# A recurrence kernel: its first slots in another order, and one turn of carries behind the log of a denominator

## The chip, the cores and the metric

The kernel runs on one core of a Trainium2 chip. The metric is the device time of one execution in microseconds; of the kernel before, four runs have a median of 294.04 us (293.59 to 295.41). The profile shows one execution, which took 294.22 us; the instructions in it span 292.5 us.

## The reference

The inputs are `k` and `v`, both [16, 2048, 256] in float32, and two vectors `w` and `u` of length 256. For each of 16 batches and 256 channels a sum with decay runs over 2048 steps, kept in a form that cannot overflow:

```python
for t in range(seq_len):
    kk, vv = k[b, t, :], v[b, t, :]
    ww = u + kk
    qq = np.maximum(pp, ww)
    e1, e2 = np.exp(pp - qq), np.exp(ww - qq)
    output[b, t, :] = (e1 * aa + e2 * vv) / (e1 * bb + e2 + 1e-08)
    ww = pp - w + kk
    qq = np.maximum(ww, kk)
    e1, e2 = np.exp(ww - qq), np.exp(kk - qq)
    aa, bb, pp = e1 * aa + e2 * vv, e1 * bb + e2, qq
```

(Two statements are put on one line here in places.) Without the scaling by `pp`, `aa` is a decayed sum of exp(k)*v, `bb` the same sum of exp(k), and an output is a quotient of the two with the present step weighted by exp(u).

## The kernel before

**Tiling.** Time is cut into a head of 32 steps and 16 chunks of 126 (two halves of 63). A chunk lies on 126 partitions, one step on each, and is done in four pieces of four batches. The head is done in two pieces, `n` = 2 and 3, in which three groups of batches are stacked on 96 partitions. In all there are 66 pieces, numbered `n`: 0 and 1 are half of chunk 0, 2 and 3 the head, 4 and 5 the rest of chunk 0, 6 to 9 chunk 1, and so on.

**What is done with a piece.** `load` (L111) brings k through SP or POOL's queue and `load_v` (L136) brings v through POOL's, converted to bf16. `round_k` (L309, VectorE) copies k into a tile[...]. `logs` (L318, TensorE) multiplies it by two "step matrices" (NLE and NLZ, for the head NLEh and NLZh), which gives all exponents of the piece, X. `exps` (L339, ScalarE) takes their exponentials, `times_v` (L350, VectorE) multiplies them by v into the other half of the same tile, `ez`. `sums` (L375, TensorE) adds the piece to the totals of its chunk. Some slots later `den` (L549, TensorE) forms the denominators by triangular matrices (Lh and Lf) and identities (Id, It), `log_den` and `invert` (L561, L568, ScalarE) turn them into reciprocals, `num` and `mult` (L573, L585) form numerators and multiply, and `store` (L591, POOL's queue) writes.

**Carries.** When the totals of a chunk are complete, a chain of small operations, each put in a slot by the table PLANS (L625), turns the totals (`turn_sums`), takes logs, updates the state, and makes the carries into the chunk. `turn_carries` (L502) transposes them on TensorE into a PSUM bank of tag "den"; `inject` (L507) casts them to bf16 on VectorE (L509) and issues four DMAs of 8 KB on SP's queue (L513), which write them into rows 126 and 127 of the chunk's `ez` tiles; the first two go to the tile of the chunk's first two pieces. From piece 4 on `den` reads these rows. For chunk 1 the turn is in slot 12 at "p4" and the injection in slot 13 at "d0".

**Order.** Each engine works in the order in which instructions are written (K, L35, pins it). The main loop (L666) has a slot for each `n`: it starts the load of piece n+6 (`AHEAD`), takes the exponentials of n, rounds k of n+1, and later in the slot forms the logs of n+1, `times_v(n)` and `sums(n)`; small jobs run where `small_work(n, "d0")` and the like stand. `out_at` (L663) gives the slot in which a piece's denominators are formed: 6 slots later for the head, 10 for pieces 0 and 1, 9 for all others. So slots 8 to 11 serve pieces 2, 3, 0 and 1, slot 12 none, and slots 13, 14 and 15 pieces 4, 5 and 6. Until the end phase there is one PSUM buffer of tag "den"; `den`, `turn_sums` and `turn_carries` take it in turn. TensorE's `idle` matmuls on zeros fill gaps in the first nine slots. k and v each have six buffers, so that a load waits for the `round_k` or the `times_v` of the piece six before.

The constants of the head's step matrices and of the output matrices are built on VectorE in slots 0 to 2 (`matrices_for_head`, `matrices_for_outputs`, `matrices_for_outputs_of_head`, `more_matrices_for_outputs`).

Of the kernel before, what the change touches and what calls it, by code (L numbers as in the profile page):

```python
# [22 lines left out]
def kernel(  # L23
# [11 lines left out]
    def K(ins):  # L35

        block, e, new = nc.cur_bb.bb, ins.ins.engine, []
        for i in reversed(block.instructions):
            if i.engine == e:
                new.append(i)  # L40
                if i.name == pinned.get(e):
                    break
        for a, b in zip(new[1:], new):
            tc.add_manual_dep(b, a.name, mybir.DependencyInfo(
                mybir.DependencyClass.NoSync, mybir.DependencyReason.DATA), reason="order")
        pinned[e] = new[0].name
        return ins

    PE, DVE, SC, POOL, SP = nc.tensor, nc.vector, nc.scalar, nc.gpsimd, nc.sync
# [9 lines left out]
    NH = NG * GB  # L59
# [36 lines left out]
    def is_head(n):  # L96
        return pairs[n][0] < 0
# [5 lines left out]
    def tiles_of(n):  # L103
        return 1 if pairs[n] == (-1, 1) else 2
# [6 lines left out]
    def load(n):  # L111
        kr = kpool.tile([128, 4, Dm], F32, tag="kr", name="kr")
        vr = vpool.tile([128, 4, Dm], BF16, tag="vr", name="vr")
        kr_of[n], vr_of[n] = kr, vr
        c, p = pairs[n]
        if is_head(n):
            load_head(n, SP, kr, k)
        else:
            t0 = T0 + c * TC
            r = min(128, T - t0)  # L120
            K((SP if n < 2 else POOL).dma_start(  # L121
                out=kr[0:r, :, :], in_=k[4 * p:4 * p + 4, t0:t0 + r, :].rearrange("n t d -> t n d")))
            if n >= 2:
                load_v(n)

    def load_head(n, eng, t, x):
        p = pairs[n][1]
        for g in (0, 2, 1):
            b = 6 * g + 4 * p
            e = min(b + 2 * tiles_of(n), B)  # L130
            if b < e:
                K(eng.dma_start(out=t[g * GB:(g + 1) * GB, 0:e - b, :],
                                in_=x[b:e, 0:T0, :].rearrange("n t d -> t n d")))
# [39 lines left out]
    M1, I1, IO, IOh = [matrix(x, F32) for x in ("M1", "I1", "IO", "IOh")]  # L173
# [28 lines left out]
    NLE, NLZ, NLEh, NLZh = [matrix(x, F32R) for x in ("NLE", "NLZ", "NLEh", "NLZh")]  # L202

    def step_matrices(E, Z, rows, N, io):
        cw, cu = cc[:, rows:rows + 1], cc[:, rows + 1:rows + 2]
        K(DVE.scalar_tensor_tensor(E[:, 0:N], io[:, 0:N], cw, M1[:, 0:N], ALU.mult, ALU.add))
        K(DVE.scalar_tensor_tensor(Z[:, 0:N], I1[:, 0:N], cu, E[:, 0:N], ALU.add, ALU.add))
        K(DVE.tensor_scalar(E[:, 0:N], E[:, 0:N], cw, None, ALU.add))
# [51 lines left out]
    def matrices_for_sums():  # L260

        K(DVE.tensor_add(Ir[:, 0:16], I1[:, 0:16], I1[:, 32:48]))
        K(DVE.tensor_add(Ir[:, 16:32], I1[:, 64:80], I1[:, 96:112]))
        K(DVE.tensor_add(Ir[:, 32:48], I1[:, 16:32], I1[:, 48:64]))
        for t in (OHE, OHV):
            fill(t, 0.0)
            fill(t[0:HS, 8:9], 1.0)
            K(DVE.tensor_single_scalar(t[:, 16:17], cc[:, 4:5], 2.0, op=ALU.mult))
        K(DVE.tensor_copy(OHE[:, 24:33:8], cc[:, 2:4]))

    def matrices_for_head():
        step_matrices(NLEh, NLZh, 0, NH, IOh)
        for f in (NLEh, NLZh):
            head_blocks(f)
            fill(f[:, NH:128], 0.0)
        for g in range(NG):
            fill(NLEh[g * GB:(g + 1) * GB, NH + g:NH + g + 1], 0.5)
        K(DVE.tensor_single_scalar(NLEh[96:98, NH:NH + NG], cc[96:98, 0:1].broadcast_to([2, NG]),
                                   -0.5 * GB, op=ALU.mult))
# [29 lines left out]
    def round_k(n):  # L309
        r = NH if is_head(n) else TC  # L310
        i = 2 * tiles_of(n)
        if is_head(n):
            KM[n] = kmh.pop(0)
        else:
            KM[n] = kms[n % 2]
        K(DVE.tensor_copy(KM[n][0:r, 0:i, :], kr_of.pop(n)[0:r, 0:i, :]))  # L316

    def logs(n):  # L318
        kr = NH + 2 if is_head(n) else 128


        if n == HALVES:
            psx[0] = log_banks("psx")
        if n < HALVES:
            X = [psx[0].tile([128, 2, D], F32, tag=f"X{q}", name=f"X{q}") for q in range(2)]
        else:
            t = psx[0].tile([128, 2, 2, D], F32, tag="X", name="X")
            X = [t[:, 0], t[:, 1], t]
        km = KM.pop(n).rearrange("p (i n) d -> p i (n d)", i=2)
        for q, m in enumerate((NLEh, NLZh) if is_head(n) else (NLE, NLZ)):  # L330
            for i in range(tiles_of(n)):
                K(PE.matmul(X[q][:, i, :], m[0:kr, :], km[0:kr, i, :], start=True, stop=True))  # L332
        X_of[n] = X
# [16 lines left out]
    def times_v(n):  # L350
        ez = ez_of(n)
        i = tiles_of(n)
        r = NH if is_head(n) else TC
        vb = vr_of.pop(n)[:, 0:2 * i, :].rearrange("p (i n) d -> p i (n d)", n=2)
        K(DVE.tensor_mul(ez[0:r, 1:4:2], ez[0:r, 0:4:2],  # L355
                         vb[0:r].unsqueeze(1).broadcast_to([r, 2, i, D])))
# [261 lines left out]
    def at(slot, where, f, *args):  # L618
        later.setdefault((slot, where), []).append((f, args))

    def small_work(n, where):
        for f, args in later.pop((n, where), []):
            f(*args)
# [23 lines left out]
    for c in range(-1, NST):  # L647
        for slot, where, f, *args in PLANS["head" if c < 0 else "first" if c == 0 else
                                           "last" if c + 1 == NST else "steady"]:

            if f is copy_sums and 0 < c < NST - 1:
                where, args = "d1", (DVE,)
            at(last_of[c] + slot, where, f, c, *args)
    at(0, "d1", matrices_for_head)
    at(0, "d2", matrices_for_outputs)
    at(1, "d2", matrices_for_outputs_of_head)
    at(2, "d2", more_matrices_for_outputs)

    matrices_for_sums()
    round_k(0)  # L660
    logs(0)

    out_at = {n + (LAG - 3 if is_head(n) else LAG + 1 if n < 2 else LAG): n for n in range(NP)}  # L663
# [2 lines left out]
    for n in range(NP + LAG + 1):  # L666

        q, qi, qp = out_at.get(n), out_at.get(n - 1), out_at.get(n - 2)
        late = ([qp] if n == LATE else []) + [qi] if n >= LATE else []
        if n >= LATE:  # L670
            qp = None
        live, more, out_q, out_qi, out_qp = n < NP, n + 1 < NP, q is not None, qi is not None, qp is not None
        if n == NP:
            widen()
        if n + AHEAD < NP:
            load(n + AHEAD)
        small_work(n, "a3")
        if live:
            exps(n)
        small_work(n, "d0")  # L680
        if more:
            round_k(n + 1)
        small_work(n, "p0")
        if out_qp:
            num(qp, 0)
            if n > NP:
                num(qp, 1)
        small_work(n, "d1")
        small_work(n, "a0")
        small_work(n, "p1")  # L690
        if n == NP:
            num(qp, 1)
        if out_qi and qi < NP - 1:
            invert(qi)
        small_work(n, "a2")
        if out_q:
            if q not in DEN:
                den(q)
            if n == NP + 1:

                den(q + 1)
            if q < NP - 1:
                log_den(q)
            else:
                for i in range(2):
                    log_den(q, i, i + 1)
                    invert(q, i, i + 1)
        for x in late:
            num(x, 0)
            num(x, 1)  # L710
            mult(x, 0)
            mult(x, 1)
            store(x)
        if out_qp:
            mult(qp, 0)
        small_work(n, "d2")
        small_work(n, "d3")
        small_work(n, "a4")
        if more:
            logs(n + 1)  # L720
        if n < HALVES + 1:
            idle(psd if n < 5 else psn, 2)
        if live and out_qp:
            num(qp, 1)
        small_work(n, "p3")
        if live:
            times_v(n)
            sums(n)
        if n < HALVES + 1 and n != 4:
            idle(psd if n < 4 else psn, 2)  # L730
        small_work(n, "p2")
        small_work(n, "d4")
        if out_qp:
            mult(qp, 1)
            store(qp)
        small_work(n, "d5")
        small_work(n, "p4")
        small_work(n, "a1")
# [31 lines left out]
```

## Time and profile before

| | |
|---|---|
| median of four runs | 294.04 us (293.59 to 295.41) |
| profiled execution; span of its instructions | 294.22 us; 292.5 us |
| ScalarE (ACT) busy | 265.7 us, 91% of the span |
| VectorE (DVE) busy | 256.0 us, 88% |
| TensorE (PE) busy | 254.7 us, 87% |
| GpSimd (POOL) busy, most of it issuing DMAs | 161.4 us, 55% |
| HBM traffic | 68.12 MB read, 34.05 MB written |

In the profile, L12 is line 12 of the kernel; a group or a timeline row gives start and length in us, engine, line, operation, what it writes `<-` what it reads, the shape, how many (x), and in brackets how long the engine stood idle before it and who ended that. SPq and POOLq are the queues that issue DMAs. The landing of a DMA is the time of the last update of its semaphore. A table of windows gives the busy time of each engine in a stretch, with the number of instructions.

### The profile page before, as it was taken

The numbers are of one execution on the slowest core, as the hardware profiler recorded it, in microseconds if no ns is written. First come the engines' busy times: TensorE is split into PE (matmuls) and PEld (weight loads), VectorE is DVE, ScalarE is ACT, GpSimd is POOL, SyncE is SP. The second block draws the span as 40 slices with busy tenths as digits, with TensorE's granted clock in tenths as the row PEclk, the third lists the DMA queues.
The fourth block names the chain that finished last, engine by engine and source line by source line (L and its number), as shares of the span: only waits on it lengthen the run. The fifth ranks groups of instructions, "written<-read, shape, count | busy, mean of one in ns | idle before, by whom it ended". The sixth has DMA issues, their size and how long they took to land.

```text
span 292.5 us, 4134 instructions
## 1 busy us (share of the span) xinstructions
PE 254.7 (87%) x1210; PEld 118.9 (41%) x1210; DVE 256.0 (88%) x529; ACT 265.7 (91%) x298; POOL 161.4 (55%) x229
## 2 busy tenths in 40 slices
PE   7589988888989898989989899989899898988950
PEld 3235444443434443434444344444344444433420
DVE  5878899889999999999999999999999999978760
ACT  7569889799999999999999999999999999998970
POOL 8895447656555665555666555666465652212430
PEclk9999999999999999999999999999999999999995
DMA  5999999999999999999999999999999999445884
GB/s 180 228 265 298 308 306 274 223 331 326 319 322 329 338 327 333 318 335 344 341 324 327 334 337 339 336 323 332 336 318 335 324 296 284 148 148 185 280 251 148
DMA packets 58203, 85.95 MB, mean 294 GB/s; under 512 B 6746, under 2 KB 42066, under 8 KB 58180
## 3 DMA queue, kind: packets, MB, share of 16 engines
q0 software_dynamic: 52960, 83.04, 102.8%
q1 hardware_dynamic: 4922, 2.36, 3.2%
q10 hardware_dynamic: 298, 0.27, 0.3%
q8 instruction: 10, 0.16, 0.2%
q14 instruction: 13, 0.11, 0.1%
HBM read 68.12 MB, written 34.05 MB: 349 GB/s over the span
## 4 chain that ended last, share of the span: by engine, by line
DVE 39%; DMA 22%; PE 20%; issue 8%; ACT 8%; SPq 1%; DVEq 0%; ACTq 0%
DMA vr<-in_v_dram 17%; DVE ez L355 14%; DVE rd L589 10%; PE num L579 6%; DVE km L316 5%; PE X L332 4%; PE den L554 4%; ACT rd L566 3%; PE tot L386 3%; DMA ez<-row 2%; PE den L404 2%; DMA kr<-in_k_dram 2%; ACT ez L346 1%; DVE S L428 1%; ACT ez L348 1%
## 5 line engine op out<-in xcount | busy, mean ns | idle before, releaser
L348 ACT ACTIVATE ez<-X 128x2048 bf16<-128x2048 f32 x58 | 108.7, 1874 | 0.1
L143 POOL DMA_DIRECT2D vr<-in_v_dram x64 | 48.6, 759 | 80.3 <-DVE ez L355 42.2
L589 DVE TENSOR_TENSOR rd<-num,rd 128x512 f32<-128x512 f32 (+2 forms) x131 | 88.4, 682 | 4.4 <-ACT rd L571 3.6
L355 DVE TENSOR_TENSOR ez<-ez,vr 126x2048 bf16<-126x2048 bf16 (+1 forms) x66 | 79.7, 1207 | 2.1 <-ACT ez L346 2.1
L609 POOL DMA_DIRECT2D out_dram<-rd x63 | 55.0, 872 | 39.5 <-issue 10.6
L566 ACT ACTIVATE rd<-den 128x1024 f32<-128x1024 f32 (+3 forms) x67 | 66.9, 999 | 4.6 <-PE den L554 2.5
L571 ACT ACTIVATE rd<-rd 128x1024 f32<-128x1024 f32 (+3 forms) x67 | 69.3, 1035 | 0.3
L579 PE MATMUL num<-ez,LfN 128*128 128x512 bf16 (+1 forms) x128 | 49.2, 384 | 7.6 <-DVE rd L589 7.6
L332 PE MATMUL X<-km,NLE 128*128 128x512 f32 x128 | 50.3, 474 | 2.3 <-DVE km L316 1.9
L316 DVE CAST km<-kr 126x1024 fp32r<-126x1024 f32 x64 | 48.7, 761 | 2.2 <-DMA kr<-in_k_dram 2.2
L579 PE MATMUL num<-ez,IdN 126*128 126x512 bf16 (+1 forms) x131 | 49.8, 380 | 0.0
L121 POOL DMA_DIRECT2D kr<-in_k_dram x62 | 47.9, 773 | 1.4 <-DMA vr<-in_v_dram 0.5
L332 PE MATMUL X<-km,NLZ 128*128 128x512 f32 x128 | 40.4, 397 | 0.0
L554 PE MATMUL den<-ez,Id 126*128 126x512 bf16 (+1 forms) x131 | 39.1, 378 | 0.0
L554 PE MATMUL den<-ez,Lf 128*128 128x512 bf16 (+1 forms) x128 | 38.0, 378 | 0.6 <-DMA ez<-row 0.6
L386 PE MATMUL tot<-ez,OHV 126*32 126x512 bf16 x128 | 25.2, 384 | 6.4 <-DVE ez L355 6.3
L332 PEld LDWEIGHTS X<-km,NLE 128*128 128x128 f32 x128 | 23.0, 189 | 13.2 <-issue 1.4
L332 PEld LDWEIGHTS X<-km,NLZ 128*128 128x128 f32 x128 | 23.9, 188 | 6.1 <-ACT ez L346 0.6
L386 PE MATMUL tot<-ez,OHE 128*32 128x512 bf16 x128 | 25.2, 390 | 0.0
L579 PEld LDWEIGHTS <-LfN 128*128 128x128 bf16 (+1 forms) x128 | 12.3, 96 | 22.9 <-issue 20.5
L346 ACT ACTIVATE ez<-X 128x1024 bf16<-128x1024 f32 (+1 forms) x16 | 14.7, 971 | 6.8 <-PE X L332 6.6
L554 PEld LDWEIGHTS <-Lf 128*128 128x128 bf16 (+1 forms) x128 | 12.3, 98 | 19.3 <-issue 7.9
(113 smaller groups left out, 211.3 us busy)
## 6 DMA issues: line engine op xcount, KB each, us to landing
out_dram<-rd POOLq DMA_DIRECT2D x60, 512.0 KB, 7.4
kr<-in_k_dram POOLq DMA_DIRECT2D x58, 512.0 KB, 8.1
vr<-in_v_dram POOLq DMA_DIRECT2D x60, 256.0 KB, 7.2
kr<-in_k_dram POOLq DMA_DIRECT2D x4, 504.0 KB, 8.9
out_dram<-rd POOLq DMA_DIRECT2D x3, 504.0 KB, 6.1
kr<-in_k_dram SPq DMA_DIRECT2D x2, 512.0 KB, 4.8
vr<-in_v_dram POOLq DMA_DIRECT2D x4, 252.0 KB, 8.2
ez<-row SPq DMA_DIRECT2D x62, 8.0 KB, 5.7
```

The source lines that it names most:

```text
L143: K(POOL.dma_start(out=vr_of[n][0:r, :, :], in_=v[4 * p:4 * p + 4, t0:t0 + r, :].rearrange("n t d -> t n d")))
L316: K(DVE.tensor_copy(KM[n][0:r, 0:i, :], kr_of.pop(n)[0:r, 0:i, :]))
L332: K(PE.matmul(X[q][:, i, :], m[0:kr, :], km[0:kr, i, :], start=True, stop=True))
L348: K(SC.activation(ez_of(n)[:, 0:4:2], X[2][:, :, 0:i, :], ACT.Exp))
L355: K(DVE.tensor_mul(ez[0:r, 1:4:2], ez[0:r, 0:4:2], vb[0:r].unsqueeze(1).broadcast_to([r, 2, i, D])))
L386: K(PE.matmul(TOT[c][y:y + 32], m[0:r, :], ez_of(n)[0:r, q, i, :], start=n == first_of[c], stop=n == last_of[c] or (head and i == 1), tile ...
L554: K(PE.matmul(d[:, i, :], m[0:r, :], ez_of(n)[0:r, q, i, :], start=q == 0, stop=q == 2, skip_group_check=True))
L566: K(SC.activation(RD[n][0:r, a:b, :], DEN[n][0:r, a:b, :], ACT.Ln, scale=RS))
L571: K(SC.activation(RD[n][0:r, a:b, :], RD[n][0:r, a:b, :], ACT.Exp, scale=-1.0))
L579: K(PE.matmul(d, m[0:r, :], ez_of(n)[0:r, q, i, :], start=q == 1, stop=q == 3, skip_group_check=True))
L589: K(DVE.tensor_mul(RD[n][0:r, i, :], NUM.pop((n, i))[0:r, :], RD[n][0:r, i, :]))
L609: K(eng.dma_start(out=out[4 * p + a:4 * p + b, t0:t0 + r, :].rearrange("n t d -> t n d"), in_=o[0:r, a:b, :]))
```

## The change

- The k of pieces 4 and 5 is loaded through SP's queue, as that of pieces 0 to 3 is, and no longer through POOL's.
- The head's step matrices are built before the loop, after `round_k(0)`; `round_k(1)` follows them, also before the loop.
- In slots 0 to 3, k of piece n+2 is rounded, at the place after "d2"; in slot 4 none is; from slot 5 on it is n+1 at the old place.
- `sums(0)`, `sums(1)` and `sums(2)` are issued a slot later, ahead of `times_v` of that slot; slot 3 issues `sums(2)` and `sums(3)`.
- The three functions that build the output matrices move from "d2" of slots 0, 1 and 2 to "d4" of slots 4, 5 and 6.
- `den(4)` is issued in slot 12 at "p2", where it was issued in slot 13; its log stays in slot 13.
- For chunk 1, `turn_carries` moves from slot 12 "p4" to slot 13 "p3", and `inject` from slot 13 "d0" to slot 13 "d4": both come behind the log of the denominators of piece 4.

```diff
@@ load
-            K((SP if n < 2 else POOL).dma_start(
+            K((SP if n in (0, 1, 4, 5) else POOL).dma_start(
@@ matrices_for_head
-        step_matrices(NLEh, NLZh, 0, NH, IOh)
@@ plans
+            if c == 1 and f in (turn_carries, inject):
+                slot, where = 4, "p3" if f is turn_carries else "d4"
+
...
     at(0, "d1", matrices_for_head)
-    at(0, "d2", matrices_for_outputs)
-    at(1, "d2", matrices_for_outputs_of_head)
-    at(2, "d2", more_matrices_for_outputs)
+    at(12, "p2", den, 4)
+    at(4, "d4", matrices_for_outputs)
+    at(5, "d4", matrices_for_outputs_of_head)
+    at(6, "d4", more_matrices_for_outputs)
 
     matrices_for_sums()
+
+    EARLY = 4
     round_k(0)
+    step_matrices(NLEh, NLZh, 0, NH, IOh)
+    round_k(1)
     logs(0)
@@ main loop
         small_work(n, "d0")
-        if more:
+        if more and n > EARLY:
             round_k(n + 1)
...
         small_work(n, "d2")
+        if n < EARLY:
+            round_k(n + 2)
         small_work(n, "d3")
...
         small_work(n, "p3")
         if live:
+            if 0 < n < EARLY:
+                sums(n - 1)
             times_v(n)
-            sums(n)
+            if n >= EARLY - 1:
+                sums(n)
```

## The prediction

> **What bounds the kernel now.** I read the windows first, to see which engine fills which stretch. Columns: length, then busy us (instructions) of PE, PE's weight loads, DVE, ACT, POOL, then clock, DMA share, GB/s.
>
> ```profile
> 8.58:31.57 22.99, 19.39 (x94) 8.89 (x95) 19.07 (x51) 15.70 (x23) 16.79 (x23) 1.00 1.24 272
> 31.57:50.20 18.63, 16.98 (x95) 8.42 (x93) 17.42 (x39) 16.98 (x21) 9.92 (x14) 1.00 1.22 301
> 50.20:62.50 12.30, 10.87 (x63) 5.46 (x61) 10.63 (x21) 10.60 (x12) 7.53 (x10) 1.00 1.07 255
> 62.50:258.00 195.50, 179.86 (x849) 84.80 (x848) 184.18 (x358) 192.00 (x211) 110.75 (x138) 1.00 1.13 320
> ```
>
> From 62.5 to 258 us ACT is busy 192.0 of 195.5 us (98%). Nothing of the change lies there; its length stays, and the change is worth the amount by which it moves the start of that stretch. Ahead of it no engine is full on its own: ACT is busy 15.7 of 23.0 us up to 31.6. So I read waits and order, first in the timelines of ACT and DVE.
>
> ```profile
> 14.42 1.94 ACT L346 ACTIVATE ez<-X 128x1024 bf16<-128x1024 f32 x2 [3.02 <-PE X L332]
> 20.13 1.94 ACT L346 ACTIVATE ez<-X 128x1024 bf16<-128x1024 f32 x2 [2.20 <-PE X L332]
> ```
>
> ```profile
> 7.88 0.71 DVE L316 CAST km<-kr 126x1024 fp32r<-126x1024 f32 x1 [1.31 <-DMA kr<-in_k_dram]
> 11.71 1.22 DVE L355 TENSOR_TENSOR ez<-ez,vr 126x2048 bf16<-126x2048 bf16 x1
> ...
> 22.10 1.23 DVE L355 TENSOR_TENSOR ez<-ez,vr 126x2048 bf16<-126x2048 bf16 x1 [1.65 <-ACT ez L346]
> 30.44 1.22 DVE L355 TENSOR_TENSOR ez<-ez,vr 126x2048 bf16<-126x2048 bf16 x1
> ```
>
> ACT waits for exponents of pieces 2 and 4. These wait behind the sums of the piece before on PE, which wait for DVE, which from 7.88 to 20.45 runs without a gap, matrices included. From about 34 us the chain is DVE nearly throughout (17.42 of 18.63 us busy in the window, 93%). Last, the chain around slot 13:
>
> ```profile
> 52.05 0.30 DVE row L509
> 52.35 0.02 SPq L513
> 52.38 0.03 issue
> 52.41 0.50 SPq L513
> 52.91 0.04 issue
> 52.95 7.14 DMA ez<-row
> 60.09 0.14 issue
> 60.23 1.04 PE den L554 x4
> 61.29 1.03 ACT rd L566
> ```
>
> Denominators of piece 6 (slot 15) wait for the second carry row of chunk 1 before they start, and ACT's full stretch begins behind them. In the list of waits of 49 to 63 us two lines matter:
>
> ```profile
> ACT rd L566 <- PE den L554: 1.7, 2, 1.5
> PE den L554 <- DMA ez<-row: 0.6, 1, 0.6
> ```
>
> ACT stands 1.5 us before the log of piece 4 (53.58), and PE 0.56 us for the row. The carries have no slack at all, which the change's move of them spends.
>
> [...] v of piece 0 lands 8.0 us after its issue beside SP's loads of k (11.34), v of piece 1 then 1.27 us later, alone. [...] the small rows on SP take 5.7 us at the median here, so the measurement is used. [...] an early job on DVE that waits for data holds all behind it, as DVE's 1.31 us for k of piece 1 shows.
>
> **Part 1, the start.** The deadline is `times_v(7)`, before at 30.44, behind which DVE's dense stretch and slot 8 stand. From 8.58 to 31.57 DVE is busy 19.07 us and idle 3.92, of which 3.04 are its listed waits (1.65, 0.44, 0.43, 0.36, 0.16). The head's step matrices (0.30+0.32+0.27, 0.95 with gaps) go into the 1.31 us that DVE waits for k of piece 1: gain 0.95, at no cost as that wait covers them. The output matrices are 1.1 us (10.62 to 11.7), 0.9 (13.45 to 14.35) and 1.5 (15.85 to 17.4), 3.5 us in all; they move on the same engine ahead of the same deadline, so they gain nothing unless they fill idle time. Hence the most to gain is 0.95+3.04 = 4.0 us, less new idle time. I walk DVE through the new order with these durations (round 0.6 to 0.7, v product 1.15 to 1.2).
> Fills 8.6 to 9.7; k of piece 2 lands at 10.18 (its last group): idle 0.6; rounded by 10.95; v of piece 0 lands at 11.34: idle 0.45; product until 12.6; k of piece 3 rounded by 13.0. Now v of piece 1. It landed at 12.61 with SP's ring empty from 11.17 on. After the change SP's ring goes on with k of 4 and 5, 1.4 us of transfer each (k of 5 landed 1.38 after v of 4). That both rings shared is unseen for such loads. Bounds: 12.6 if v loses nothing, 15.4 if both k's go first (12.6+2.8). From 7.78 to 11.17 SP moved its 512 KB of heads while v moved most of 512 KB read: I take two fifths for POOL, so v of 1 needs 1.25/0.4 us: lands about 14.4; idle 1.45. Product until 15.6; k of 4 until 16.3; v of 2 (about 16.5): idle 0.2; product 17.7; k of 5 18.35; v product 3 19.0. PE meanwhile: sums 1 16.1, two idles 16.6, logs of 4 to 17.6; ACT's exponentials of 4 at 17.2 to 19.1 (before 20.13), so ACT's 3.0 and 2.2 us do shrink. Product 4 19.15 to 20.35, then the first matrices to 21.4, k of 6 to 22.1, idle 0.4 for the turn of the head's sums, product 5 to 23.9, matrices to 24.8, k of 7, product 6 to 26.65, state and the last matrices (0.2+1.5) to 28.35, split, k of 8 to 29.3, offsets to 29.9, product 7. That is 30.44-29.9 = 0.55 earlier. By idle time: 4.0-(0.6+0.45+1.45+0.2+0.15+0.4) = 0.75. I take **-0.6**; with v at 12.6 the idle sum without the 1.45 and 0.2 says -2.4, of which the exponentials of pieces 5 and 6, which PE then times, hold some 0.6 back: -1.8; with v at 15.4 (1.0 later) less what idle time it takes up further on, about +0.2. So ACT's early lead of 3 us at piece 4 goes: the matrices stand in slots 5 and 6 before the rounding that slots 6 to 8 need.
> POOL has two issues fewer (0.79 and 0.94) and later loads come some 0.5 us sooner; k of 7 had 1.6 us in hand (landed 24.15, used 25.78), so that is not on the path. SP has two issues more at about 5.4 to 6.9 us, with nothing queued behind them until 35.59. Delayed sums cost PE nothing: it has them ready, and the totals are first read in slot 4.
>
> **Part 2, slots 12 and 13.** `den(4)` starts at 51.2, behind sums 12, where PE now waits 0.54 for the carries; num(1) at 51.9; log of 4 at about 52.1 instead of 53.58; ACT's next exponentials at 53.85 instead of 54.51, since logs of 14 still wait for PE. DVE, though, keeps its times: it loses a cast (0.2) and a wait (0.33) at 52, and waits 0.4 for num(1). `times_v(13)` is at 53.55 to 54.7. So pieces 14 and 15, which DVE and the turn of sums at 58.6 time, gain nothing, and `den(6)` is ready at about 59.7 as now (60.23-0.56).
> The cast of the carries comes behind log of 4, num(1,1), the turn (54.45 to 54.65) and, on DVE, behind `times_v(13)`: 54.75 instead of 52.05, +2.7. SP's second issue is then at 55.65 instead of 52.95. The row took 7.14 us there; second rows elsewhere take 4.7 to 7.9, the next two (other half of chunk 1) 6.55 and 6.19. With 6.2 it lands at 61.85, against 60.09: **+1.75**, all of it on PE, as `den(6)` waits already; queued behind it on PE are logs of 16, num(4,1) and sums 15, and ACT's log of 6 waits. With 5.3 it is +0.9, with 7.2 +2.8. Were the row not to bind, the part would give -0.56 at best. What ACT recovers later is its idle time behind that (3.5 us in 195), say -0.1.
>
> **Sum** against the profiled execution: 294.22-0.6+1.75-0.1 = 295.3. It stands 0.18 over the median, so 295.1 on that scale; I say **295.0**, own range 293.8 to 296.2. Under 0.5% (1.47 us: 292.57 to 295.51) a measurement of this kernel can hardly tell from no change.
>
> **Rivals.** *A, slower: SP's k loads starve v.* If v of piece 1 lands at 15.4 or the two rings together move less than POOL's alone, the start gives +0.2 to +0.8 and the total is 295.9 to 297. It decides from v of piece 1 at about 14.8 on. For it: 8.0 us for the first v beside SP's loads. Against: those were loads to 32 partitions. *B, the start gains in full.* v hardly later, -1.8, row in 5.5 us (+1.05): 293.2. For it: POOL's transfers never leave a gap. *C, faster: neither binds.* Early exponentials keep their 3 us at slot 8, because DVE fits matrices into waits that I did not count, and the row's latency falls below 5 us[...]: -2.5 and +0.3, 291.8. For it: ACT's 6.2 us of waits in 13 to 26 us; against it: DVE busy 17.4 of 18.6 us right after. *D, the change does not do what it says:* the log of 4 still waits 1.5 us, because `den(4)` in slot 12 waits for the bank; but its last reader (log of 1) ended at 46.7. This is in A and B.
>
> **Chances.** My forecast 0.45, of it two thirds within the bound, a third slower; A 0.2, slower; B 0.2, within; C 0.15, faster. So faster 0.15, within 0.50, slower 0.35. The range 292.3 to 297.0 leaves out most of C and the end of A.
>
> **What would show it.** ACT's first exponentials of piece 4 near 17.2; `times_v(7)` near 29.9; v of piece 1 landing near 14.4 and DVE waiting for it; log of 4 without its 1.5 us wait; carries cast 2.7 us later in the slot, and PE's wait for the row in slot 15 grown from 0.6 to over 2 us. The forecast is wrong if that wait stays below 1 us, or if slot 8 starts over 1.5 us earlier.

## The result and the profile after

The changed kernel has a median of 295.37 us, the kernel before 294.08 us beside it: a ratio of 1.003 [1.0015, 1.0044], +0.9 us. The ratio is taken over the fast executions alone (those within 1.5% of the quickest of their kernel), so it differs a little from that of the two medians. Two repeats on other chips gave 1.0048 [1.0025, 1.0072] and 1.0051 [1.003, 1.0072]. Its profiled execution took 292.55 us (span 290.8), the quickest of all those of this kernel, 2.8 us under the median; so the profile of a repeat (295.34 us, span 293.5), which stands near the median, is read beside it. Below, "the repeat" is that one.

The windows of the changed kernel, cut at the same points of the work as those of before; the columns are the same (length, then busy us and instructions of PE, weight loads, DVE, ACT, POOL, then clock, DMA share, GB/s).

```profile
8.36:29.73 21.37, 18.89 (x92) 8.78 (x92) 17.58 (x48) 16.19 (x24) 15.98 (x22) 1.00 1.28 277
29.73:48.59 18.86, 16.97 (x96) 8.58 (x96) 17.28 (x39) 17.17 (x20) 10.86 (x15) 1.00 1.25 307
48.59:62.14 13.55, 11.27 (x63) 5.52 (x61) 10.94 (x21) 10.89 (x12) 7.54 (x10) 1.00 1.12 291
62.14:256.70 194.56, 178.21 (x849) 84.93 (x848) 183.06 (x357) 191.73 (x211) 111.60 (x138) 1.00 1.13 317
```

The first stretch is 1.62 us shorter, the second 0.23 us longer, the third, with slot 13 and the wait for the row in it, 1.25 us longer, and the last, in which the change does nothing, 0.94 us shorter; 0.2 us ahead of the first and 0.4 us behind the last make up the rest of the 1.7 us between the two spans. The first went further than the forecast said, the third is near it, and the last moved although it was held fixed.

ACT's timeline of the changed kernel, the exponentials of pieces 2 and 4:

```profile
11.98 3.13 ACT L345 ACTIVATE ez<-X 128x1024 bf16<-128x1024 f32 x4 [0.53 <-PE X L331]
...
16.49 1.94 ACT L345 ACTIVATE ez<-X 128x1024 bf16<-128x1024 f32 x2 [1.38 <-PE X L331]
```

The waits of 3.02 and 2.20 us are 0.53 and 1.38; piece 4 starts at 16.49 instead of 20.13. DVE's timeline, with the product of piece 1, `times_v(7)` and the cast of the carries:

```profile
13.77 1.23 DVE L354 TENSOR_TENSOR ez<-ez,vr 126x2048 bf16<-126x2048 bf16 x1 [1.04 <-DMA vr<-in_v_dram]
...
28.60 1.22 DVE L354 TENSOR_TENSOR ez<-ez,vr 126x2048 bf16<-126x2048 bf16 x1
...
53.18 0.28 DVE L508 CAST row<-den 128x128 bf16<-128x128 f32 x1
```

v of piece 1 landed at 13.68 and DVE stood 1.04 us for it; `times_v(7)` is 1.84 us earlier than before. The cast of the carries is 1.13 us later in time, and 2.73 us later once the earlier start (1.60 us, at slot 8) is taken off.

Last, the log of piece 4 on ACT, the denominators of piece 6 on PE, and, from the list of waits of 45 to 66 us, PE's wait for the row (the columns there are sum, number and longest):

```profile
50.65 1.02 ACT L565 ACTIVATE rd<-den 128x1024 f32<-128x1024 f32 x1 [0.20 <-PE den L553]
```

```profile
59.84 0.59 PE L553 MATMUL den<-ez,Lf 128*128 128x512 bf16 x2 [1.85 <-DVE S L427]
```

```profile
PEld L553 <- DMA ez<-row: 2.3, 1, 2.3
```

The log's wait of 1.52 us is gone (0.20). PE's idle time before `den(6)` rose from 0.56 to 1.85 us. The row in the list says what it is: the timeline names an old event of DVE as the last releaser, but the weight load of the same matmul waits for the row of carries.

In the repeat near the median the same place looks worse. Its chain, from the product of piece 13 on:

```profile
51.60 1.14 DVE ez L354
52.74 0.21 DVE row L508
...
53.55 7.79 DMA ez<-row
...
61.48 1.44 PE den L553 x4
```

The second row takes 7.79 us here and PE stands 3.98 us for it; and `den x4` takes 1.44 us where before it took 1.04. That second difference is what the windows of the same execution explain, us by us (clock is the third column from the end):

```profile
62.00:63.00 1.00, 1.00 (x4) 0.64 (x3) 0.00 (x0) 0.04 (x1) 0.00 (x0) 0.50 1.17 284
63.00:64.00 1.00, 1.00 (x4) 0.72 (x3) 0.00 (x0) 1.00 (x2) 0.00 (x0) 0.50 1.43 261
64.00:65.00 1.00, 1.00 (x4) 0.18 (x2) 0.00 (x0) 0.63 (x3) 0.00 (x0) 0.50 1.11 373
```

After its wait PE works at half clock for over three us. It is full in all of them, DVE does nothing, and ACT next to nothing in the first: the lost speed is on the path.

To compare runs I use the starts of ACT's exponentials of single slots, each as a shift in us against the profile of before: slot 8 (behind the start), slot 15 (ahead of the row), slot 16 (behind it) and slot 65 (the last). What the row costs is the step from 15 to 16, what the long stretch gives is the step from 16 to 65.

| kernel | slot 8 | slot 15 | slot 16 | slot 65 |
|---|---|---|---|---|
| changed, first profile | -1.60 | -1.99 | -0.39 | -1.32 |
| changed, repeat near the median | -2.20 | -2.46 | +2.13 | +1.16 |
| changed, third chip | -0.90 | -1.27 | +1.43 | +0.19 |

Four shifts in a row below are those of these four slots.

### The profile page after: what moved, and what is told of

The parts are those of the page before. It is cut to its first block, busy times and chain, and to the rows that moved or that the text cites. A ratio compares the mean times of both kernels' runs of the same rounds, so it can differ in the third digit from the quotient of the medians.

```text
span 290.8 us, 4132 instructions
## 1 busy us (share of the span) xinstructions
PE 253.6 (87%) x1210; PEld 119.2 (41%) x1210; DVE 254.3 (87%) x529; ACT 265.9 (91%) x298; POOL 162.2 (56%) x227
## 4 chain that ended last, share of the span: by engine, by line
DVE 38%; DMA 21%; PE 17%; issue 10%; ACT 10%; SPq 1%; POOL 0%; DVEq 0%; POOLq 0%; ACTq 0%
DVE ez L354 14%; DVE rd L588 11%; DMA out_dram<-rd 9%; DMA vr<-in_v_dram 7%; PE num L578 6%; DVE km L315 5%; DMA kr<-in_k_dram 5%; ACT rd L565 4%; PE den L553 3%; ACT ez L347 3%; PE X L331 3%; PE tot L385 2%; PE den L403 2%; ACT rd L570 1%; DVE S L427 1%
## 5 line engine op out<-in xcount | busy, mean ns | idle before, releaser
L608 POOL DMA_DIRECT2D out_dram<-rd x63 | 56.3, 893 | 41.3 <-issue 13.2
L121 POOL DMA_DIRECT2D kr<-in_k_dram x60 | 46.4, 773 | 5.1 <-DMA kr<-in_k_dram 2.1
L315 DVE CAST km<-kr 126x1024 fp32r<-126x1024 f32 x64 | 47.1, 736 | 1.8 <-DMA kr<-in_k_dram 1.8
L553 PEld LDWEIGHTS <-Id 126*128 126x128 bf16 (+1 forms) x131 | 12.7, 97 | 15.7
```

What stands on the lines that cost most here:

```text
L553: K(PE.matmul(d[:, i, :], m[0:r, :], ez_of(n)[0:r, q, i, :], start=q == 0, stop=q == 2, skip_group_check=True))
L608: K(eng.dma_start(out=out[4 * p + a:4 * p + b, t0:t0 + r, :].rearrange("n t d -> t n d"), in_=o[0:r, a:b, :]))
```

## The experiments

**The changed kernel again**, beside the first three experiments on one chip.

> The changed kernel once more, beside the parts of it. Theory A (two opposed parts: an earlier start, worth 0.6 to 1.6 us, and a later carry row in slot 13, costing 1.2 to 1.8 us): again 0.5 to 1.3 us slower than the kernel before at the median, and in the profile PE waits 1.5 us or more for the row in slot 15. Rival B (the parts do not add up; what differs is how the long stretch after slot 16 falls, where copies on VectorE take 0.68 or 0.8 to 1.0 us): the start of slot 16 is not later than before in the profile, and the stretch from slot 16 to the end is longer than before by 1 us or more.

Measured: 295.65 us against 293.96, 1.0048 [1.0025, 1.0072]. Its profile is the one shown above.

**One part at a time.** The start alone leaves the three lines on slot 13 out of the changed kernel; slot 13 alone puts just these into the kernel before:

```diff
+            if c == 1 and f in (turn_carries, inject):
+                slot, where = 4, "p3" if f is turn_carries else "d4"
...
+    at(12, "p2", den, 4)
```

> Only the part in the first slots (k of pieces 4 and 5 through SP, k rounded two slots ahead, sums behind, matrices in slots 4 to 6); slots 12 and 13 as before. Theory A: slot 8 starts 1.6 us earlier, as in the changed kernel's profile, and the row still follows by 7 us, so the whole is 0.6 to 1.6 us faster than before. Rival B: the gain is lost in the long stretch, the whole within 0.5 us of before.

> Only the part in slots 12 and 13 (denominators of piece 4 in slot 12, turn and injection of chunk 1's carries behind their log); the first slots as before. Theory A: the log of piece 4 comes 1.5 us sooner, the row's cast 2.7 us later, PE waits about 2 us for the row in slot 15, and the whole is 1.2 to 1.8 us slower than before. Rival B: within 0.5 us of before or faster by 0.5, as ACT's wait of 1.5 us in slot 13 is gone.

Measured: the start alone 291.79 us, 0.9904 [0.9871, 0.9937], shifts -1.42, -1.38, -1.61, -2.82. Slot 13 alone 296.77 us, 1.0087 [1.0056, 1.0119], shifts -0.12, -0.51, +2.58, +2.88. Against the 293.96 us of the kernel before beside them these are -2.2 and +2.8 us, both larger than was expected (up to 1.6 and 1.8). So the two parts have opposite signs and are each two to three us in size: the small result is a difference of two large terms. Two views of slot 13 alone, PE's and ACT's timelines:

```profile
61.83 1.01 PE L554 MATMUL den<-ez,Lf 128*128 128x512 bf16 x2 [2.36 <-DMA ez<-row]
```

```profile
63.73 1.02 ACT L566 ACTIVATE rd<-den 128x1024 f32<-128x1024 f32 x1 [3.08 <-PE den L554]
```

`den(6)` starts 1.60 us later than before (60.23), but ACT's log of it 2.44 us later (61.29): two matmuls take 1.01 instead of 0.59 us, and the 0.84 us between the two delays is lost after the row has landed.

The start alone also shows the long stretch by itself: its shift goes from -1.61 at slot 16 to -2.82 at slot 65, while slot 13 alone has +2.58 and +2.88.

**The turn as early as the bank allows.** Is it the late row that costs, or the new order of the log and the turn? In slot 13 the turn goes to "d2" and the injection to "d3", still behind the log of piece 4, but ahead of the product of v:

```diff
-                slot, where = 4, "p3" if f is turn_carries else "d4"
+                slot, where = 4, "d2" if f is turn_carries else "d3"
```

> The changed kernel with the turn of chunk 1's carries straight behind the log of piece 4 on PE (ahead of the logs of piece 14) and the injection ahead of the v product of piece 13 on VectorE. Theory A: the row is cast 1.1 us earlier than in the changed kernel and lands as much earlier, PE's wait in slot 15 falls to about 0.8 us, and the time is 0.7 to 1.1 us below the changed kernel's. If the row is not what costs the time: no change, or 0.9 us slower, as logs of 14 come that much later.

Measured: 291.83 us, 0.9931 [0.9895, 0.9967]; shifts -1.64, -1.59, -0.85, -1.33. The second row is issued at 52.90 and lands at 59.24. PE's timeline:

```profile
59.38 0.59 PE L553 MATMUL den<-ez,Lf 128*128 128x512 bf16 x2 [1.24 <-DMA ez<-row]
```

The step at the row falls to 0.74 us, and the clock stays at 1.00 behind it. With the order kept and the row sooner, the loss is nearly gone: the row's lateness is the cause. The median is 3.8 us under that of the changed kernel on the same chip, where 0.7 to 1.1 was expected: against the repeat the row is cast about 1.2 us sooner once the starts are taken off, takes 6.35 instead of 7.79 us from issue to landing (its flight, below), and is not followed by the low clock. How much of the flight's difference is chance, a single profile of each cannot tell.

**PE kept busy while it waits.** Eight matmuls on zeros stand ahead of `den(6)` in slot 15; the row is as late as in the changed kernel.

```diff
+    at(15, "p1", idle, psd, 8)
```

> The changed kernel with eight idle matmuls on zeros on PE in slot 15 ahead of the denominators of piece 6, where PE waits for the carry row; nothing else. In the changed kernel run again PE waited 3.98 us there and the granted clock then stood at 0.50 for some 3.5 us (den to exponentials of 16: 3.2 us instead of 2.3). Theory A1 (the row's lateness costs 1.6 to 3.7 us, and the lowered clock 0.9 more in most runs): the clock stays at 1.00, and the median falls by 0.5 to 0.9 us against the changed kernel run again (295.65). Theory A2 (the row alone): no change within 0.3 us.

Measured: 294.03 us, 0.9993 [0.9964, 1.0022]; shifts -1.28, -1.67, +2.17, +1.72. In this profile the row landed at 62.27, so the profiled execution (295.61 us) gains nothing to be seen, while the median is 1.6 us under the changed kernel's of another chip. That did not decide it, and so both kernels were run once more, on one chip.

> The changed kernel, as the reference on one chip for the next: 0.3 to 0.5% slower than before. Theory A1: in the profile, when PE waits 2.3 us or more for the row, the clock stands at 0.50 right after.

> The kernel of e4 (eight idle matmuls on PE in its wait in slot 15), now on one chip with the changed kernel. Theory A1 (the clock's fall costs 0.9 us in most executions): 0.5 to 0.9 us below the changed kernel. Theory A2 (only the row): within 0.3 us of it. On the first look the medians lay 1.6 us apart, on two chips: if that holds here, more than the clock is at work.

Measured: the changed kernel 295.73 us, 1.0051 [1.003, 1.0072]; with PE kept busy 294.01 us, 0.9997 [0.9978, 1.0016], 1.7 us less, where 0.5 to 0.9 was expected; shifts of the latter -1.84, -2.21, +1.23, -0.03. Its step at the row is no smaller in this profile (3.44 us against 2.70), since the row's flight took 7.48 instead of 5.6 us; what the profiles show is the clock behind the landing. In both profiles PE stands idle for 1.8 us right ahead of `den(6)`; in the second the matmuls on zeros fill the time before that. The changed kernel, PE's timeline and then its windows:

```profile
60.51 1.01 PE L553 MATMUL den<-ez,Lf 128*128 128x512 bf16 x2 [1.81 <-DVE S L427]
```

```profile
61.00:62.00 1.00, 1.00 (x5) 0.44 (x3) 0.84 (x1) 0.00 (x0) 0.00 (x0) 0.50 1.02 406
```

The same two views with PE kept busy:

```profile
57.75 1.89 PE L219 MATMUL idle<-zeros 128*128 128x512 bf16 x8
...
61.45 0.59 PE L553 MATMUL den<-ez,Lf 128*128 128x512 bf16 x2 [1.82 <-DMA ez<-row]
```

```profile
62.00:63.00 1.00, 1.00 (x6) 0.75 (x4) 0.00 (x0) 0.48 (x1) 0.00 (x0) 1.00 1.12 320
```

1.01 us at clock 0.50 against 0.59 us at 1.00. From the landing of the row to the exponentials of slot 16 it takes 3.31, 3.42 and 3.59 us where the clock falls (the repeat, slot 13 alone, the third chip), and 2.44 us where it does not (before, the first profile after, the early turn, both runs with PE kept busy): the fall costs 0.9 to 1.15 us in place.

How common is it? Of 62 executions of the changed kernel (chosen as for the ratios) 57 have a mean clock below 0.986 (median 295.43 us, the other five 293.63), while with PE kept busy 31 of 36 lie at or above it (median 293.93; the other five 296.0). A mean clock does not say where in the kernel it fell, and 63 of 101 executions of the kernel before lie below 0.986 too. But the two kernels compared differ by the eight matmuls alone, so the difference between them is due to these. The first profile after, with 0.988, is one of the few in which the clock held. The rest of the 1.7 us, some 0.6 to 0.8, is no more than the intervals of the two ratios (0.2%, 0.6 us, each way) allow by chance; if it is more, its cause was not found.

**The start: loads of k by POOL.** The forecast had SP's loads of k of pieces 4 and 5 as the cost of the start, since they hold back v. The start alone, with these two loads left on POOL's queue:

```diff
-            K((SP if n in (0, 1, 4, 5) else POOL).dma_start(
+            K((SP if n < 2 else POOL).dma_start(
```

> The start part alone, as in e1, but with k of pieces 4 and 5 on POOL's queue as before. My step in the forecast (SP's loads hold back v of piece 1): v of 1 lands at 12.6 instead of 13.7 and slot 8 starts 0.5 to 1.2 us earlier than in e1. Theory R (the two transfers fewer on POOL shift which of POOL's issues meets the copies of k on VectorE; in e1 two of eight copies in the long stretch are shorter, 0.68 instead of 0.74 and 0.88, 0.25 us per eight pieces): those copies are 0.74 and 0.88 again, and 1.2 to 1.5 us of e1's lead are lost between slots 20 and 56.

Measured: 295.25 us, 1.0024 [1.0001, 1.0046]; shifts +2.19, +2.19, +3.13, +3.23. DVE's timeline, the rounding of k of pieces 4 and 5:

```profile
15.52 0.87 DVE L315 CAST km<-kr 126x1024 fp32r<-126x1024 f32 x1 [1.36 <-DMA kr<-in_k_dram]
...
19.27 0.69 DVE L315 CAST km<-kr 126x1024 fp32r<-126x1024 f32 x1 [1.76 <-DMA kr<-in_k_dram]
...
25.39 0.36 DVE L410 COPY tsum<-den 128x192 f32<-128x192 f32 x1 [2.04 <-PE den L403]
```

DVE stands 3.1 us for the two, and everything queued behind waits with it. The two loads are issued at 10.95 and 12.87 us here, behind those of v on POOL's queue, and at 5.37 and 5.9 us on SP's in the start alone. So the loads on SP are not the price of the start but its condition. What they give is less sure in size. At slot 8 it is 3.6 us (-1.42 against +2.19, on different chips), but this profiled execution is 2 us over the median of its kernel, and a second loss is in it: PE, idle for 1.9 us until 20.62, takes 1.71 us for the four matmuls of logs at 21.81, where it takes 1.19 us for those at 32.04, and DVE stands 2.04 us for the totals that PE turns (the last line). By the medians the difference is 3.5 us; against the 13 of its executions with a mean clock of 0.986 or more (median 294.2 us) it is 2.4.

**The start: matrices in their old place.** The start alone, with the three functions that build the output matrices back in slots 0 to 2:

```diff
-    at(4, "d4", matrices_for_outputs)
-    at(5, "d4", matrices_for_outputs_of_head)
-    at(6, "d4", more_matrices_for_outputs)
+    at(0, "d2", matrices_for_outputs)
+    at(1, "d2", matrices_for_outputs_of_head)
+    at(2, "d2", more_matrices_for_outputs)
```

> The start part alone, as in e1, but with the output matrices built in slots 0, 1 and 2 as before. In e1 VectorE waits 1.13, 0.34, 1.11 and 0.51 us for transfers between 9 and 17 us and has 2.7 us of matrices in slots 4 to 6. By the sum of idle time the first two matrices (about 1.8 us) fit into those waits and the third does not: slot 8 starts 0.5 to 1.3 us earlier than in e1. If it is the later place of the matrices that gives e1 its lead: slot 8 starts 1 to 2 us later than in e1.

Measured: 290.92 us, 0.9869 [0.9832, 0.9905], the lowest median of all kernels here; shifts -2.06, -2.06, -2.26, -3.18. What the matrices had to fill is seen in DVE's timeline of the start alone, where they come late:

```profile
10.42 0.69 DVE L315 CAST kmh<-kr 96x1024 fp32r<-96x1024 f32 x1 [1.13 <-DMA kr<-in_k_dram]
...
14.12 1.22 DVE L354 TENSOR_TENSOR ez<-ez,vr 126x2048 bf16<-126x2048 bf16 x1 [1.11 <-DMA vr<-in_v_dram]
```

Those 2.2 us of waits for transfers take up work that is put there, and slots 4 to 6 are spared it: 0.64 us earlier at slot 8 (on another chip), as expected. So the move of the matrices is no gain. That it costs something is not shown by the times: the interval overlaps that of the start alone (0.9871 to 0.9937).

**Log of piece 4 early and carries early.** The turn of carries takes the "num" bank for chunk 1, so that it can stay in slot 12 although `den(4)` is there too:

```diff
-        d = bank("num", [128, D]) if wide else bank("den", [128, 2, D])[:, 0]
+        d = bank("num", [128, D]) if wide or c == 1 else bank("den", [128, 2, D])[:, 0]
...
-            if c == 1 and f in (turn_carries, inject):
-                slot, where = 4, "p3" if f is turn_carries else "d4"
```

> The changed kernel with den(4) in slot 12 as changed, but with the turn of chunk 1's carries back in slot 12 and the injection back at the head of slot 13, the turn in the PSUM bank of tag num, so that it waits for no log. Theory A: the row is cast as early as in e1 (about 50.6), PE waits under 0.6 us for it, ACT's wait of 1.5 us in slot 13 is gone; time at or below that of e1 (291.79), by 0 to 0.6 us, and 3 to 4 us below the changed kernel. If den(4) in slot 12, and not the row, is what costs the time: within 1 us of the changed kernel.

> The changed kernel with the turn of chunk 1's carries in slot 12 in the bank of tag num and the injection at the head of slot 13 (as in e7), and with the output matrices in slots 0, 1 and 2 (as in e6). Theory A: the two gains add: 0.3 to 0.6 us below e7 and 0 to 0.6 below e6, some 290.5 us, 1.2% below the kernel before. If they share one wait: no better than e6 (290.9).

Measured: 291.38 us, 0.9895 [0.9854, 0.9935], shifts -1.70, -1.48, -1.66, -2.40; and, with the matrices in their old place as well, 291.09 us, 0.9889 [0.9868, 0.991], shifts -2.04, -1.81, -2.00, -2.59. The row now is issued at 51.52 and lands at 56.13, so PE never waits for it. But the earlier log of piece 4 brings nothing that can be measured beside the start alone (0.9904) or the start with early matrices (0.9869). ACT's wait of 1.5 us for the log is gone, and another stands in its place. From the list of waits of 45 to 70 us of the first of the two:

```profile
ACT ez L347 <- PE X L331: 1.3, 1, 1.3
```

This wait is ahead of the exponentials of slot 14, which wait for their exponents from PE; in the start alone there is none. The two gains do not add, and the simpler kernel with the matrices first is at least as quick.

**Only the two loads on SP.** To find what shortens the long stretch, the kernel before with this one line:

```diff
-            K((SP if n < 2 else POOL).dma_start(
+            K((SP if n in (0, 1, 4, 5) else POOL).dma_start(
```

> The kernel before with k of pieces 4 and 5 on SP's queue, and nothing else. Theory R (two transfers fewer on POOL shift its issues against the copies of k): no gain up to slot 16 within 0.5 us, then 0.25 us per eight pieces, 1.2 to 1.5 us by the end, so 0.4 to 0.5% faster. If the shift comes from the new order of the first slots and not from POOL's count of transfers: the copies stay at 0.74 and 0.88 us, and the time is within 0.3 us of before. My step in the forecast (SP's loads hold v back): slot 8 starts up to 1 us later.

Measured: 292.95 us, 0.9955 [0.9937, 0.9974]; shifts -0.57, -0.57, +0.43, -0.82. The step of 1.0 us at the row has nothing to do with slot 13, which is as before: the row's flight took 8.1 us in this profile, against 7.14. From slot 16 on it gains 1.25 us, as the changed kernel does (0.93, 0.97, 1.24 in its three profiles) and as the start alone does (1.21); the other kernels with the two loads on SP gain 0.45 to 1.26 there. The two with POOL's loads gain nothing (slot 13 alone loses 0.30, the start with POOL's loads 0.10). DVE's groups of 62 to 256 us say where; the columns after the count are busy us and mean ns of one. Before, and then with the two loads on SP:

```profile
L316 DVE CAST km<-kr 126x1024 fp32r<-126x1024 f32 x49 | 37.7, 770 | 0.0
```

```profile
L316 DVE CAST km<-kr 126x1024 fp32r<-126x1024 f32 x49 | 36.3, 740 | 0.0
```

1.4 us fewer over 49 roundings of k. The same mean is 740 ns in the changed kernel and 742 in the start alone, but 766 with slot 13 alone and 773 in the start with POOL's loads. It is 739 to 743 in all kernels with the two loads on SP, also in those that gain 0.45 us only, so not all that the roundings save reaches the end. The roundings differ by what POOL does meanwhile. Timeline of before at one of the longer ones, and of the changed kernel at the same piece:

```profile
87.09 0.75 POOL L143 DMA_DIRECT2D vr<-in_v_dram  x1 [1.11 <-DVE AB L472]
...
87.46 0.88 DVE L316 CAST km<-kr 126x1024 fp32r<-126x1024 f32 x1
```

```profile
86.94 0.68 DVE L315 CAST km<-kr 126x1024 fp32r<-126x1024 f32 x1
...
87.32 0.75 POOL L143 DMA_DIRECT2D vr<-in_v_dram  x1 [1.85 <-DVE rd L588]
```

The rounding that begins within POOL's issue of a load of v takes 0.88 us; the one begun ahead of that issue takes 0.68. In the profile of before 28 of the 49 roundings begin within an issue of a load of v and take 0.73 to 0.94 us, some 0.49 us more than what is left of that issue (0.24 to 0.45); the other 21, of which 17 begin within the issue of a store, take 0.68 or 0.69. In the changed kernel 17 begin within an issue of a load of v (0.81 to 0.94 us). Two of every eight roundings are quicker in the changed kernel, one by some 0.05 us (0.73 or 0.74 to 0.68 in most cases) and one by 0.20 us (0.88 to 0.68), 0.25 us per eight pieces. In the two timelines above the rounding was lengthened by 0.20 us, not by the 0.38 us of the issue that were left at its start, and POOL's issue took 0.75 us in both. What lies behind this no run here shows. That two loads fewer on POOL shift the later issues against the roundings is shown by this run; by what way they do so stays open.

## Why the prediction was right, and where its steps were not

The total was right: 295.0 forecast, 295.4 to 295.7 measured, inside its own range of 293.8 to 296.2, with neither a gain nor a large loss. But this was luck: errors of opposite sign cancelled. By the medians of the parts the start gives 2.2 us, where 0.6 was forecast, and slot 13 costs 2.8, where 1.65 was. One of the forecast's own signs of being wrong came true as well: slot 8 starts over 1.5 us earlier in two of three profiles (-1.60 and -2.20). By the steps:

- **Part 1, the walk of DVE to `times_v(7)`, -0.6.** Mis-sized: -1.84 at `times_v(7)` in the first profile, and at slot 8 -1.60, -2.20 and -0.90 in three. Two terms account for it. v of piece 1 landed at 13.68, not at 14.4: so the share of two fifths for POOL beside SP was too low. And the output matrices took 2.73 us in slots 4 to 6 (0.89+0.82+1.02), not the 3.5 of slots 0 to 2; single operations that took 0.41 to 0.53 us there took 0.21 to 0.36. That goes with what was left of POOL's issues at their starts, 0.38 to 0.51 us there and at most 0.36 here, but was not tried by itself. The walk's shape held: exponentials of piece 4 at 16.49 (forecast 17.2), and that early lead of 3.64 us gone to 1.60 by slot 8 since the matrices stand in slots 5 and 6.
- **"SP's k loads hold v back" as the cost of the start.** As far as v goes, right in sign (1.07 us later than before). As a verdict on the loads, wrong: with k on POOL the start is not faster than the kernel before (1.0024), since k of pieces 4 and 5 comes too late to be rounded two ahead. The forecast compared only v's landing and did not price the other case, k on POOL behind v. It gave the earlier issue on SP no size; for these two loads it is 5.6 and 7 us (5.37 and 5.9 against 10.95 and 12.87). Rival A did not come about: v of piece 1 landed at 13.68, ahead of its 14.8.
- **Part 2, the log of piece 4 and the cast.** Right: wait of the log 1.52 to 0.20, ACT's exponentials of slot 14 some 0.6 us earlier, DVE with the times it had; cast +2.73 (forecast +2.7).
- **Part 2, the row, +1.75.** Taken as the delay of `den(6)` against the shift of slot 8, the row cost 1.2 in the first profile (59.84 is 0.39 earlier than 60.23, where slot 8 is 1.60 ahead), 1.2 on the third chip (+0.28 and 0.90), and with slot 13 alone 1.7 (+1.60 and 0.12). The repeat had 3.45 (+1.25 and 2.20), with a row of 7.79 us. So the term was well sized for most profiles, but the upper bound of 2.8 was too low: it took the longest flight seen at that place (7.14), and SP's issue alone came to 1.71 us in the repeat.
- **A term that was not there: the clock.** The sum ended when the row landed, as if PE then worked at the speed of before. In the two repeats it works at half clock for over three us, +0.9 to 1.15. With it the step from slot 15 to 16 was +4.6 and +2.7 in the repeats, instead of 1.75.
- **"Its length stays".** Wrong: the last stretch lost 0.9 to 1.25 us in the changed kernel, and something in every kernel with the two loads on SP, where two of eight roundings of k are quicker since POOL's issues come at other times. The forecast took ACT's 98% for a fixed length, but ACT's idle time there (3.5 us of it before, 2.8 in the first profile after) still follows DVE, which is argued from the roundings and not tried by itself. The -0.1 for recovery is not what happened.

For the repeat the terms read -2.46 (all up to slot 15, with the 0.3 us that the earlier log of piece 4 gives), +3.7 (row, against that), +0.9 (clock), -1.0 (long stretch): +1.1, as its profile has (295.34 against 294.22). Rival B's -1.8 for the start was the better figure, but not its row; C's total is that of the start alone (291.79), but its mechanism is not: slot 8 keeps 1.4 us there and not 3, and 1.2 us come from the long stretch. D did not occur.

**What stays open.** The ratios of the two parts give 0.9904 x 1.0087 = 0.9990, and both together measure 1.003 to 1.005: 0.4 to 0.6% more. The intervals of the two parts are 0.3% wide each way, so most of this may be noise. The repeat's longer flight of the row (7.79 us against 6.1 with slot 13 alone) goes that way, but three profiles do not say how the flights of all other executions are spread. With the first profile alone, which neither has the low clock nor a long flight, the change would have looked like a gain of 1.7 us.

The version with the lowest median is the start alone with the matrices in their old place, 290.92 us: 1.3% under the kernel before. The start alone and the two kernels with the turn in the other bank lie within its interval.

## What to carry to other kernels

When a small result comes out of a large edit, run its parts by themselves first: here -2.2 and +2.8 us were hidden in +0.9, and the best version was one part less. A small transfer that an engine waits for should be issued as early as its data permits, since what it delays is not only its own flight: in three profiles here TensorE, idle for 1.81 us or more ahead of the work that all wait for, did that work at a clock of 0.50, and matmuls on zeros in that gap took 1.7 us off the median. A stretch in which one engine is 98% busy is not of fixed length, if another engine's durations depend on who issues at the same time: here it lost 0.9 to 1.25 us in the changed kernel, where roundings of 0.73 and 0.88 us came down to 0.68.

## What the runs showed of the hardware

- **The clock after a wait.** The clock fell to 0.50 in or just behind waits of PE of 1.81, 2.36 and 3.98 us ahead of `den(6)` (the third chip, slot 13 alone, the repeat); each of the three falls lasted 3.4 us, summed over windows of 1 us. It kept 1.00 behind 1.24 us (the early turn), and behind 1.82 and 2.2 us with matmuls on zeros before them (1.89 us of them ahead of the first). The length alone doesn't decide: it also kept 1.00 behind 1.85 us in the first profile and 2.12 us in the first slots of the kernel before. Why equal waits end differently no run here shows.
- **The second row of 8 KB.** In the 14 profiles here the second row of chunk 1 landed 4.6 to 8.1 us after its issue, and SP's own issue instructions for these rows took 0.5 to 1.7 us. The flight varies by itself: it took 7.8 us in one profile of the changed kernel and 5.6 in the two others. A forecast that rests on one such flight has an error of one to two us from that alone.
- **Roundings and POOL's issues.** In the profile of before 0.73 to 0.94 us for the 28 roundings begun within POOL's issue of a load of v, 0.68 or 0.69 for the 21 others; in the changed kernel 0.81 to 0.94 for 17 and 0.68 or 0.69 for 32. Two issues moved off POOL at the start made the stretch from slot 16 on 1.25 us shorter in a profile, and the median 0.45% lower.
